# Hybrid attention layer on one core: high and low weight parts laid 128 bytes apart in their buffers

## The chip, the cores and the metric

The kernel runs on one core of a Trainium2 chip. The metric is the time of one execution on the device in microseconds (us), taken as the median of several runs. Engine names: PE is TensorE (matrix products; PEld is its weight load, a separate row of the trace), ACT is ScalarE, DVE is VectorE, POOL is GpSimd, SP issues most DMAs. A matmul has a stationary operand, which PEld loads into the array (128 columns here), and a moving operand, which is streamed through it (256, 272 or 512 columns here).

## What is computed

One decoder layer on x of 256 rows by 1024 columns, all in float32: an input RMS norm, one large product with `w_in` (1024 by 5648), block attention with 8 heads of 64, gated linear attention (GLA) with 4 heads, two branch products `w_proj_a` and `w_proj_b`, gates, the output product `w_out`, a residual and a final RMS norm.

```python
h = rms_norm(x, norm_in_g[layer])
proj = jnp.einsum('bsd,de->bse', h, w_in[layer])
(mq, mk, mv, mgate, gq, gk, gv, ggate, gfg, ga, gb) = jnp.split(proj, split_pts, axis=-1)
...
oa = oa.transpose(0, 2, 1, 3).reshape(B, S, MOBA_WIDTH) * jax.nn.silu(mgate)
ya = jnp.einsum('bse,ed->bsd', oa, w_proj_a[layer])
...
yb = jnp.einsum('bse,ed->bsd', ob, w_proj_b[layer])
merged = (jax.nn.sigmoid(ga + b_merge[layer, 0]) * ya
          + jax.nn.sigmoid(gb + b_merge[layer, 1]) * yb)
x = x + jnp.einsum('bsd,de->bse', merged, w_out[layer])
...
return rms_norm(x, norm_f_g)
```

## The kernel before

Every large product is made of three matmuls in the reduced type fp32r (helper `three`): high part by high part, high by low, low by high. Activations are split once (`xh`, `xl`; later `oah`/`oal`, `obh`/`obl`, `mh`/`ml`). Weights are split as they arrive. A weight matrix is cut into chunks of up to 1056 elements per partition. `load_to` issues a chunk's DMA on SP into one of five `raw` buffers; `split_to` makes `hi` from `raw` on ACT (line 179) and `lo` as `raw` minus `hi` on DVE (line 180), each into one of five ring buffers of `SMAX` = 1088 elements. `prefetch` keeps loads some eight chunks and splits four chunks ahead of the products.

The groups run in this order: `mg`, `gg`, `gqk`, `mq`, `mk`, `mv`, `gv`, `ga0`, `ga1`, `gb0`, `gb1`, `pa0`, `pb0`, `pa1`, `pb1`, and then the output product (`po`). There are four kinds:

- K (`mg`) and F (`gqk`, `mq`, `mk`, `ga`, `gb`, `pa`, `pb`): the weights are stationary (128 columns of `hi` or `lo`), the activations move (256 columns). An F group has two banks; each is 2 x 8 x 3 = 48 matmuls (2 x 4 x 3 = 24 for `pa` and `pb`). The order within a `three` is `hi` with `xh`, `hi` with `xl`, `lo` with `xh`.
- G (`gg`) and T (`mv`, `gv`), and `po`: the activations are stationary, and `hi` or `lo` move, 512 columns at a time (256 and 272 in `gg`, 512 and 256 in `po`).

The side work (GLA, attention, gates, merge) is written as generators; `tick`, called after every second step of an F group, starts the side steps that are due by a clock that `mm` counts from shapes alone. So the order of instructions on every engine is fixed when the kernel is built.

All large buffers lie at addresses that are equal modulo 256 bytes within their kind: every `hi` and `lo` buffer begins at 32 modulo 256 (4352 bytes each, 17 x 256), `xh`, `xl`, `oah`, `oal`, `obh`, `obl` at 224. The `raw` buffers are 4224 bytes (16.5 x 256), so consecutive ones alternate between 32 and 160 modulo 256. A row of a `gg` chunk takes 544 elements (2176 bytes, 8.5 x 256): of its two k steps the first begins at 32 and the second at 160 modulo 256.

Of the kernel before, what the change touches and what calls it, by code (L numbers as in the profile page):

```python
# [22 lines left out]
D = 1024  # L23
# [15 lines left out]
C_MQ, C_MK, C_MV, C_MG = 0, 512, 1024, 1536  # L39
C_GQ, C_GV, C_GG, C_FG, C_GA, C_GB = 2048, 2560, 3072, 3584, 3600, 4624  # L40
RANK = 16


def constants():
# [34 lines left out]
def layer(ctx, tc, x, norm_in_g, w_in, b_merge, w_fg2, b_fg, gla_g, w_pa, w_pb, w_out, norm_f_g,  # L79
# [10 lines left out]
    def mm(out, lhsT, rhs, start, stop):  # L90
        nc.tensor.matmul(out, lhsT, rhs, start=start, stop=stop)  # L91
        n = out.free_size() / 2400
        clock[0] += n if rhs.dtype == F32R else 4 * n

    def transpose(out, in_, identity):
        nc.tensor.transpose(out, in_, identity)
        clock[0] += 0.11

    def f32(ap):
        return ap.bitcast(F32)  # L100
# [11 lines left out]
    chunks = []  # L112
    groups = []

    def group(kind, name, src, c0, n, nk, step=2):
        ids = []
        if kind == "F":
            parts = [(c0 + p, 256, k0, 4) for p in range(0, n, 256) for k0 in range(0, nk, 4)]
        else:
            parts = [(c0, n, k0, step) for k0 in range(0, nk, step)]  # L120
        for c, w, k0, k in parts:
            ids.append(len(chunks))
            chunks.append(dict(src=src, c0=c, n=w, k0=k0, nk=k))
        groups.append(dict(kind=kind, name=name, ids=ids, nk=nk))

    group("K", "mg", w_in, C_MG, 512, KD, 1)
    group("G", "gg", w_in, C_GG, 528, KD)
    group("F", "gqk", w_in, C_GQ, 512, KD)
    group("F", "mq", w_in, C_MQ, 512, KD)
    group("F", "mk", w_in, C_MK, 512, KD)  # L130
# [10 lines left out]
    for half in range(2):  # L141
        for n in range(2):
            for k in range(4 * half, 4 * half + 4, 2):
                oids[n, k // 2] = len(chunks)
                chunks.append(dict(src=w_out, c0=n * 512, n=512, k0=k, nk=2))

    WMAX = 1056
    SMAX = 1088
# [20 lines left out]
    def split_to(n):  # L169
        while done[0] < min(len(chunks), n):  # L170
            c = chunks[done[0]]
            size = c["nk"] * c["n"]
            w = c["n"]
            row = w if w % 32 == 0 else 544
            hi = ring.tile([P, SMAX], F32R, name="hi", bufs=SPLIT)
            lo = ring.tile([P, SMAX], F32R, name="lo", bufs=SPLIT)
            c["hi"], c["lo"] = (t[:, :c["nk"] * row].rearrange("p (k n) -> p k n", n=row)[:, :, :w] for t in (hi, lo))
            raw = c["raw"].rearrange("p (k n) -> p k n", n=w)
            nc.scalar.copy(c["hi"], raw)  # L179
            nc.vector.tensor_sub(c["lo"], raw, f32(c["hi"]))  # L180
            done[0] += 1

    def prefetch(i):

        load_to(i + SPLIT + RAW - 2)
        split_to(i + SPLIT - 1)
# [9 lines left out]
    for k0, k1 in ((0, 1), (1, 2), (2, 4), (4, 6), (6, 8)):  # L196
# [12 lines left out]
        (ggb, gla_g.to_broadcast([P, GDV])),  # L209
        (fgw[0:RANK, :], w_fg2),  # L210
        (fgw[RANK:RANK + 1, :], b_fg),
        (sumsf, sums),
# [64 lines left out]
    for k in range(2):  # L277
        split_to(k + 1)
        x_part(k)
# [15 lines left out]
    kT = one.tile([P, HP, S], F32, name="kT")  # L295
    gfs = one.tile([P, NT, RANK], F32, name="gfs")
    gfT = one.tile([32, S], F32, name="gfT")
# [21 lines left out]
    def give(tag, n=1):  # L319
        room[tag] += n  # L320
# [42 lines left out]
    def gla():  # L363
# [4 lines left out]
        for t in range(NT):  # L368
            transpose(tr[:RANK, t * P:(t + 1) * P], gfs[:, t, :], ident)
        yield 0.6  # L370
        nc.scalar.copy(gfT[:RANK, :], tr[:RANK, :S])
        give("small")
# [3 lines left out]
        for t in range(NT):  # L376
            mm(fg[:, t, :], gfT[:RANK + 1, t * P:(t + 1) * P], fgw[:RANK + 1, :], start=True, stop=True)
        yield 0.8
# [345 lines left out]
    for g in groups:  # L724
        ids, name = g["ids"], g["name"]
        if g["kind"] == "K":
            ps = [small(f"{name}{f}") for f in range(3)] + [bank(f"{name}3", "side", 1)]
            for i in ids:
                c = chunks[i]
                k = c["k0"]  # L730
                if k == 5:
                    squares(0)
                if k == 6:
                    squares(1)
                for f in range(4):
                    fs = slice(f * P, (f + 1) * P)
                    if f == 2:
                        if k + 2 < KD:
                            x_part(k + 2)
                        split_to(i + SPLIT - 1 if k > 3 else i + 3)  # L740
                    three(ps[f][:, :S], c["hi"][:, 0, fs], c["lo"][:, 0, fs], xh[:, k, :], xl[:, k, :],
                          k == 0, k == KD - 1)
            start_side(gates_mg(ps))
        elif g["kind"] == "G":
            ps = {(t, b): (small if t and b else bank)(f"{name}{t}{b}") for t in range(NT) for b in range(2)}
            for i in ids:
                prefetch(i)
                c = chunks[i]
                for kk in range(c["nk"]):
                    k = c["k0"] + kk  # L750
# [8 lines left out]
        elif g["kind"] == "T":  # L759
            ps = [bank(f"{name}{t}") for t in range(NT)]  # L760
            for i in ids:
                prefetch(i)
                c = chunks[i]
                for kk in range(c["nk"]):
                    k = c["k0"] + kk
# [6 lines left out]
        elif g["kind"] == "F":  # L772
            src = {"pa": (oah, oal), "pb": (obh, obl)}.get(name[:2], (xh, xl))
# [18 lines left out]
            nk = g["nk"]  # L792
            per = nk // 4
            for b in range(len(ids) // per):
# [6 lines left out]
                for j in range(2):  # L801
# [3 lines left out]
                    for k in range(nk):  # L805
                        c = chunks[i + k // 4]
# [94 lines left out]
```

## Time and profile before

| | |
|---|---|
| time, median of 3 runs | 209.54 us (209.42 to 210.56) |
| time of the profiled execution | 209.73 us |
| its span, first to last instruction | 208.0 us |
| PE busy | 198.8 us, 96% |
| PEld busy | 182.4 us, 88% |
| DVE, ACT, POOL busy | 141.6, 122.6, 32.5 us |
| granted TensorE clock, mean | 0.997 |

Matmuls overlap in the trace (one is drained while the next streams), so the durations of neighbours add up to more than the time that passed. The pace of a run of matmuls is the distance of two starts, or the length of a piece of the chain divided by its count.

### The profile page before, as it was taken

To read this page: it belongs to the slowest core of one execution; us is meant where nothing else is said; L and a number is where in the kernel's file an instruction comes from. 1 tells how busy PE (TensorE), PEld (TensorE's weight loads), DVE (VectorE), ACT (ScalarE), POOL (GpSimd) and SP (SyncE) were. 2 spreads that over 40 slices of the span, in tenths; PEclk is the share of its full clock that TensorE was granted. 3 is DMA by queue.
4 is the path that set the end of the run, shared out by engine and by line. 5 is a ranking of instruction groups with operands and counts; after the bars stand their busy time and mean duration, and the time that the engine had idled before them with its cause. 6 is when DMAs were issued, how large, how long until landed. Compare 5 with 4: busy or idle time off the path is not lost.

```text
span 208.0 us, 4231 instructions
## 1 busy us (share of the span) xinstructions
PE 198.8 (96%) x1683; PEld 182.4 (88%) x1683; DVE 141.6 (68%) x261; ACT 122.6 (59%) x205; POOL 32.5 (16%) x31
## 2 busy tenths in 40 slices
PE   7999999999999999998999999999999999999970
PEld 2899999899999988775789999999999999989870
DVE  1566778969545899989765556945393959755371
ACT  4369927871999984156775629846455554552251
POOL 2000025800214540103000000200010060420011
PEclk9999999999999999999999999999999999999998
DMA  5999896594364456660343563966344584600022
GB/s 144 349 379 323 238 310 211 135 296 149 101 199 117 145 158 191 193 218 14 107 123 86 182 193 114 294 210 198 108 151 154 168 301 135 204 4 2 0 101 101
DMA packets 28501, 35.39 MB, mean 170 GB/s; under 512 B 1305, under 2 KB 21442, under 8 KB 28482
## 3 DMA queue, kind: packets, MB, share of 16 engines
q1 hardware_dynamic: 28178, 34.60, 54.1%
q10 hardware_dynamic: 304, 0.53, 0.7%
q8 instruction: 13, 0.21, 0.4%
q14 instruction: 6, 0.05, 0.1%
HBM read 34.08 MB, written 1.05 MB: 169 GB/s over the span
## 4 chain that ended last, share of the span: by engine, by line
PE 67%; DVE 11%; ACT 11%; issue 5%; DMA 2%; SPq 1%; POOLq 0%; POOL 0%; ACTq 0%; DVEq 0%
PE ga L91 11%; PE gb L91 11%; PE po L91 8%; PE gg L91 6%; PE gqk L91 6%; PE pa L91 5%; PE pb L91 5%; DVE lo L180 4%; ACT hi L179 4%; PE mg L91 3%; ACT z L700 3%; PE mq L91 3%; DMA xt<-in_x_dram 2%; PE gv L91 2%; DVE EX L417 2%
## 5 line engine op out<-in xcount | busy, mean ns | idle before, releaser
L180 DVE TENSOR_TENSOR lo<-raw,hi 128x1024 fp32r<-128x1024 f32 (+1 forms) x56 | 70.4, 1269 | 23.5 <-ACT hi L179 23.5
L179 ACT CAST hi<-raw 128x1024 fp32r<-128x1024 f32 (+1 forms) x56 | 57.7, 1048 | 21.5 <-PE po L91 6.0
L91 PE MATMUL ga<-xh,hi 128*128 128x256 f32 x64 | 18.1, 283 | 0.0
L91 PE MATMUL gb<-xh,hi 128*128 128x256 f32 x64 | 18.1, 282 | 0.0
L91 PE MATMUL gb<-xh,lo 128*128 128x256 f32 x64 | 17.9, 279 | 0.0
L91 PE MATMUL gb<-xl,hi 128*128 128x256 f32 x64 | 17.9, 279 | 0.0
L91 PE MATMUL ga<-xh,lo 128*128 128x256 f32 x64 | 17.8, 278 | 0.0
L91 PE MATMUL ga<-xl,hi 128*128 128x256 f32 x64 | 17.8, 278 | 0.0
L91 PE MATMUL po<-hi,ml 128*128 128x512 f32 (+1 forms) x40 | 13.9, 347 | 0.0
L91 PE MATMUL po<-lo,mh 128*128 128x512 f32 (+1 forms) x40 | 13.8, 346 | 0.0
L91 PE MATMUL po<-hi,mh 128*128 128x512 f32 (+1 forms) x40 | 13.7, 343 | 0.0
L91 PEld LDWEIGHTS ga<-xh,hi 128*128 128x128 f32 x64 | 12.1, 189 | 0.5 <-issue 0.5
L558 ACT ACTIVATE sm<-sm,mx 128x128 f32<-128x128 f32 (+1 forms) x16 | 7.1, 444 | 8.7 <-DVE mx L553 8.6
L91 PEld LDWEIGHTS gb<-xh,lo 128*128 128x128 f32 x64 | 12.1, 189 | 0.0
L91 PEld LDWEIGHTS gb<-xh,hi 128*128 128x128 f32 x64 | 12.1, 189 | 0.0
L91 PEld LDWEIGHTS ga<-xl,hi 128*128 128x128 f32 x64 | 12.0, 188 | 0.0
L91 PEld LDWEIGHTS gb<-xl,hi 128*128 128x128 f32 x64 | 12.0, 188 | 0.0
L91 PEld LDWEIGHTS ga<-xh,lo 128*128 128x128 f32 x64 | 12.0, 188 | 0.0
L511 POOL TENSOR_TENSOR s<-s,mhalf 128x4 f32<-128x4 f32 x2 | 2.3, 1172 | 54.6 <-DVE s L510 54.6
L624 POOL TENSOR_TENSOR m<-m,sa 128x512 f32<-128x512 f32 x4 | 7.0, 1743 | 23.9 <-DVE m L622 22.0
L91 PE MATMUL mg<-xh,hi 128*128 128x256 f32 x32 | 10.3, 321 | 0.0
L91 PE MATMUL mg<-xl,hi 128*128 128x256 f32 x32 | 9.5, 296 | 0.0
(197 smaller groups left out, 605.7 us busy)
## 6 DMA issues: line engine op xcount, KB each, us to landing
raw<-in_w_in_dram SPq DMA_DIRECT2D x36, 512.0 KB, 3.7
raw<-in_w_out_dram SPq DMA_DIRECT2D x8, 512.0 KB, 4.8
raw<-in_w_in_dram SPq DMA_DIRECT2D x4, 528.0 KB, 6.0
first<-in_w_in_dram SPq DMA_DIRECT2D x8, 256.0 KB, 5.5
raw<-in_w_proj_a_dram SPq DMA_DIRECT2D x4, 512.0 KB, 3.5
raw<-in_w_proj_b_dram SPq DMA_DIRECT2D x4, 512.0 KB, 4.4
xt<-in_x_dram SPq DMA_DIRECT2D x3, 256.0 KB, 5.7
late<-in_norm_f_g_dram SPq DMA_DIRECT2D x1, 512.0 KB, 5.0
```

Of the source, the lines that this page charges most:

```text
L91: nc.tensor.matmul(out, lhsT, rhs, start=start, stop=stop)
L179: nc.scalar.copy(c["hi"], raw)
L180: nc.vector.tensor_sub(c["lo"], raw, f32(c["hi"]))
L417: nc.vector.tensor_mul(e, e, halves(src, LEVELS[l], which))
L511: nc.gpsimd.tensor_tensor(s4, s4, mhalf, op=OP.pow)
L558: nc.scalar.activation(sm[i][:, cs], sm[i][:, cs], AF.Exp, bias=mx[:, i, t:t + 1], scale=0.125, accum_out=den[:, i, t:t + 1])
L624: nc.gpsimd.tensor_add(m, m, cut(sg["ga"]))
L700: nc.scalar.copy(z[i:i + 32], p2[i ^ 32:(i ^ 32) + 32])
```

## The change

Two offsets are given to each chunk, in elements, for `hi` and for `lo`: (0, 32) is kind A, (32, 0) is B, (0, 0) is C and (32, 32) is D; 32 elements are 128 bytes. Groups `gqk`, `mk`, `ga1` get A; `mq`, `ga0` get B; `gb0` and `gb1` alternate A and B from chunk to chunk; `gv` gets D; `mg`, `gg`, `mv`, `pa`, `pb` and the output product stay at C. The buffers keep their size and place; only the views `c["hi"]` and `c["lo"]`, which ACT and DVE write and PE reads, begin 128 bytes later. No instruction is added, removed or moved.

```diff
+KINDS = {'gqk': 'A', 'mq': 'B', 'mk': 'A', 'ga0': 'B', 'ga1': 'A', 'gb0': 'M', 'gb1': 'M', 'gv': 'D'}
+
+
+def shift(name, n):
+    kind = KINDS.get(name, "C")
+    if kind == "M":
+        kind = "AB"[n % 2]
+    return dict(A=(0, 32), B=(32, 0), C=(0, 0), D=(32, 32))[kind]
...
-            chunks.append(dict(src=src, c0=c, n=w, k0=k0, nk=k))
+            chunks.append(dict(src=src, c0=c, n=w, k0=k0, nk=k, shift=shift(name, len(chunks))))
...
-                chunks.append(dict(src=w_out, c0=n * 512, n=512, k0=k, nk=2))
+                chunks.append(dict(src=w_out, c0=n * 512, n=512, k0=k, nk=2, shift=(0, 0)))
...
-            c["hi"], c["lo"] = (t[:, :c["nk"] * row].rearrange("p (k n) -> p k n", n=row)[:, :, :w] for t in (hi, lo))
+            c["hi"], c["lo"] = (t[:, d:d + c["nk"] * row].rearrange("p (k n) -> p k n", n=row)[:, :, :w]
+                                for t, d in zip((hi, lo), c["shift"]))
```

## Rows read from the trace of the kernel before

**Rows 1.** Page: busy time, share of span, instructions; chain's shares by engine.
```profile
PE 198.8 (96%) x1683; PEld 182.4 (88%) x1683; DVE 141.6 (68%) x261; ACT 122.6 (59%) x205; POOL 32.5 (16%) x31
PE 67%; DVE 11%; ACT 11%; issue 5%; DMA 2%; SPq 1%; POOLq 0%; POOL 0%; ACTq 0%; DVEq 0%
```

**Rows 2.** Chain that ended last, in order of time: start us, us, what, count.
```profile
33.38 2.83 PE gqk L91 x24
...
46.16 5.67 PE mq L91 x48
...
51.85 0.58 ACT z L700
...
75.11 1.21 DVE lo L180
...
107.26 7.02 PE ga L91 x60
...
116.53 7.50 PE ga L91 x66
...
125.72 7.26 PE ga L91 x60
132.99 5.66 PE gb L91 x48
138.64 0.44 PE tr L96 x4
139.08 7.51 PE gb L91 x66
146.59 1.78 PE o L91 x16
148.38 9.19 PE gb L91 x78
157.57 0.44 PE tr L96 x4
158.00 5.46 PE pa L91 x48
163.46 5.44 PE pb L91 x48
```

**Rows 3.** Groups by form, 109.36 to 113.8 us: shapes, count, busy us, mean ns.
```profile
L91 PE MATMUL ga<-xh,hi 128*128 128x256 f32 x14 | 3.9, 276 | 0.0
```

**Rows 4.** The same view, 126.5 to 132.8 us.
```profile
L91 PE MATMUL ga<-xh,hi 128*128 128x256 f32 x18 | 5.1, 281 | 0.0
L91 PEld LDWEIGHTS ga<-xh,hi 128*128 128x128 f32 x18 | 3.5, 192 | 0.0
```

**Rows 5.** Timeline of PE, start us and duration us: where each gg k step begins.
```profile
22.24 0.29 PE L91 MATMUL gg<-hi,xh 128*128 128x256 f32 x1
...
23.69 0.28 PE L91 MATMUL gg<-hi,xh 128*128 128x256 f32 x1
...
25.16 0.28 PE L91 MATMUL gg<-hi,xh 128*128 128x256 f32 x1
...
26.60 0.28 PE L91 MATMUL gg<-hi,xh 128*128 128x256 f32 x1
...
28.06 0.28 PE L91 MATMUL gg<-hi,xh 128*128 128x256 f32 x1
```

**Rows 6.** Views of lines 180 and 179: duration ns min/median/max, first, last start us.
```profile
L180 DVE TENSOR_TENSOR lo<-raw,hi x56: 1207/1218/2309, 19.5 to 191.2; 128x1024 fp32r<-128x1024 f32 x52, 128x1056 fp32r<-128x1056 f32 x4
L179 ACT CAST hi<-raw x56: 1029/1049/1073, 18.4 to 190.1; 128x1024 fp32r<-128x1024 f32 x52, 128x1056 fp32r<-128x1056 f32 x4
```

**Rows 7.** Waits by engine and line: us in total, times, longest us.
```profile
DVE lo L180 <- ACT hi L179: 25.9, 19, 3.6
```

## The prediction

> **What bounds the kernel now.** I read the page's busy times first and then the chain that ended last. PE is busy for 96% of the span, and two thirds of the chain is PE's [rows 1]. In order of time the chain has three parts [rows 2]. Up to about 52 us it is PE: `mg`, `gg`, `gqk` and the first bank of `mq`. Then it passes to ACT at the first eviction of `mq` (51.85) and to DVE (one of its splits stands at 75.11), and stays there until the GLA and attention work of that stretch is through. From about 96 us to the end of `po` it is PE again, through `ga`, `gb`, `pa`, `pb`. So a nanosecond saved in a matmul counts in the first and the last part, and is given back as a wait in the middle.
>
> Next I divided the chain's PE pieces by their counts, because the change touches only where operands lie. All these matmuls have the same shape: 128 weight columns loaded, 256 columns streamed. They run at two paces. `pb` takes 5.44 us for 48, 113.3 ns each; `pa` is the same but for its first one. `gqk` takes 2.83 for 24, 117.9; `mq` 5.67 for 48, 118.1; the first piece of `gb` 5.66 for 48, 117.9; its last 9.19 for 78, 117.8. The middle piece of `gb` takes 7.51 for 66, 113.8 with its start included [rows 2]. The view by form shows the same from another side: a `ga` matmul of the quick pace lasts 276 ns, one of the slow pace 281, and in the slow stretch the load of one of the three operands lasts 192 ns instead of 188 [rows 3, 4]. I call the difference a step: 117.8 - 113.3 = 4.5 ns.
>
> What changes the pace? Not the clock (0.997 over the span), not the buffers (a run of 48 or more crosses several chunks, whose buffers rotate), and not ACT or DVE, since `pb` holds 113.3 while splits run beside it. The pace changes only where side matmuls come between: after the `tr` at 138.64 `gb` is quick, after the `o` at 146.59 slow, after the `tr` at 157.57 `pa` is quick and stays so [rows 2]. Within a run it stays, after the first few. So it looks like two ways for weight load and moving stream to fall into step with each other, or with something that serves both, and the start decides which.
>
> **Does a shift of 128 bytes matter to that?** The trace has one place where it is tried. In `gg` the moving operand starts at 32 modulo 256 in one k step and at 160 in the next. From 22.24 a step at 160 takes 1.45 us, then 1.47 at 32, 1.44 at 160, 1.46 at 32 [rows 5]: 12 matmuls are about 0.02 us shorter at 160, some 1.5 ns each, a third of a step. So PE is not blind to these 128 bytes. That is the moving operand; in the F groups it is the stationary one that the change moves, and no row tries that.
>
> **The change, part by part.**
>
> PE, F groups (kinds A, B, M). No instruction, wait or DMA is added, so the count on each queue and the order on each engine stay. In the kernel before, all three weight loads of a `three` stand in the same relation to what is streaming: weights at 32, activations at 224, modulo 256. With A the `lo` load stands 128 bytes off, one of three; with B the two `hi` loads do. A pace in which each of the three pays a step needs each to meet the same relation; with one of them moved off, I expect the slower pace to break up and the stream to fall to the quick pace, as it does by itself after some breaks. The price of that:
> - `gqk`, 96 matmuls (pieces of 24, 24 and 48 in the chain; one row stands for them), and the first bank of `mq`, 48: 144 x 4.5 ns = 0.65 us, on the path because ACT's eviction at 51.85 waits for the end of that bank [rows 2].
> - `ga` from 125.72, 60 matmuls (7.26 us: 60 at 117.8 and about 0.2 us to start), and `gb`, 48 and 78: 186 x 4.5 = 0.84 us, on the path [rows 2].
> - The quick runs (`ga` 60 at 107.26 and 66 at 116.53, `gb` 66 at 139.08; 192 matmuls) are taken to stay quick: nothing.
> - The rest of `mq` and `mk` (144 at the slower pace) lie in the ACT and DVE part: PE gets there up to 0.65 us sooner and waits. I take nothing, and keep 0.65 us as the far end should the side work follow.
>
> PE, `gv` (kind D). `hi` and `lo` move together, which is what `gg` does between its k steps: 48 matmuls x 1.5 ns = 0.07 us either way by that row, and the stage is in DVE's part of the chain, so nothing.
>
> ACT and DVE. They write and read `hi` and `lo` 128 bytes on. `raw` alternates by just these 128 bytes from buffer to buffer against `hi` and `lo`, and the median split on DVE lasts 1218 ns with a fastest of 1207, on ACT 1049 between 1029 and 1073 [rows 6]: no second level shows. (The longest on DVE, 2309 ns, are a few isolated ones.) I take nothing and keep 0.1 us both ways, since DVE's splits already wait 25.9 us in all for ACT's [rows 7] and so have slack outside the middle part. DMAs land in `raw`, which does not move.
>
> The sum is 0.65 + 0.84 = 1.49 us. The quick runs too start with a few slow matmuls (60 in 7.02 us is 0.22 us over 60 x 113.3), so I take nine tenths, 1.34 us. The profiled execution took 209.73 us, 0.19 above the median of 209.54; from its own time the sum gives 208.39, from the median 208.2. The forecast is 208.2.
>
> **A rule that speaks against the change.** The paces above are what the rows show [rows 2]. The Trainium skill, page "SBUF — State Buffer", section "Who interferes with whom", says that PE has two independent read ports, one for the moving operand and one for weight loads, and that "PE and ACT never wait on anyone". By that the place of the weights could cost PE nothing and the time would stay at 209.5. The `gg` steps speak against its strict reading; for stationary operands no row here shows it either way. It is the second case below. The page "TensorE: Matmul & The Clock Gate", section "Wait — 56ns, not 53.3ns?", puts the distance of two warm starts at N / 2.4 GHz plus about 2.5 ns; as an estimate by that page that is 109.2 ns for 256 columns, and all 522 matmuls on the path at it would give about 205.9 us. No row here shows a 256-column pace under 113.3.
>
> **The rivals.**
> 1. The shift doesn't do what it is laid out for: the pace hangs on the moving operand and on how a run starts, and the weights' place is of no matter. For it: buffers of all addresses show both paces, and a break alone changes them [rows 2]. Against it: the load that lasts 192 ns instead of 188 at the slower pace, so the weight side takes part [rows 4]. Then runs start as before, or are dealt anew: if the share of quick runs stays, 209.5; all 192 quick ones turned slow would cost 0.86 us, 210.4.
> 2. The moved relation is the dearer one. Then each load that stands 128 bytes off pays a step more, at either pace alike. A moves one of three, B two of three, about half over the groups: half of 144 + 186 + 192 = 522 is 261 x 4.5 ns = 1.17 us, 210.7. It decides from 1.05 us, that is 233 loads that pay. For it: the one row on the shift shows that the two relations differ by a third of a step [rows 5], and in `gg` that is for better from 32 to 160 against 224, which says nothing of the other operand. Against it: `pa` and `pb` run at 113.3 in the old relation, so that one is not dear in itself, and the new one would have to be dear at every start.
> 3. Only the front gains, because `ga` and `gb` are dealt anew at each of their breaks: 0.65 us, 208.9. This lies within the bound of what can be told from no change, and is counted there.
>
> **How the numbers follow.** About 0.5% (1.05 us) is what a measurement of this kernel can tell from no change. The forecast has 0.50, rivals 1 and 3 together 0.38, rival 2 has 0.12. Faster by over 0.5% (under 208.5) is the forecast, 0.50; within it 0.38; slower 0.12. The forecast's own range is 207.2 to 208.6: its low end is 209.54 less 1.49, less the 0.65 of `mq` and `mk`, less 0.07 of `gv` and 0.1 of ACT and DVE. The whole range goes from 207.2 to 210.0; it leaves out rival 2 and the upper part of rival 1.
>
> **What would show it.** In the changed profile I would divide the same chain pieces by their counts. Right: `gqk` and `mq` at 113 to 114 ns, each piece of `ga` and `gb` likewise, durations of 276 ns instead of 281, ACT's first eviction of `mq` near 51.2 instead of 51.85, `gv` and the splits as before. Wrong in the mechanism: `gqk` still at 118, so that weights' addresses don't matter; wrong in place: the front quicker and the end no earlier, if ACT or DVE takes the gain; wrong in sign: matmuls of 256 columns above 118 ns, or loads above 192. Since the pace is set anew at each break, a gain in some pieces and a loss in others is the result that would hurt the forecast most.

## The result and the profile after

The changed kernel takes 211.0 us (median of 14 runs, 209.76 to 212.44) beside 209.81 us for the kernel before in the same comparison (14 runs): a ratio of 1.0055, interval 1.003 to 1.008. Two more comparisons, told below, gave 1.0014 (0.998 to 1.0048) and 1.0039 (1.0019 to 1.0059). So the change makes the kernel slower, by 0.1 to 0.6%, which one of the three comparisons can't tell from no change; the forecast was 208.2. The profiled execution took 210.74 us, its span is 208.9, and the granted clock 0.997, as before.

The page's busy times of after (engine, busy us, share of the span, instructions) stand against [rows 1]:

```profile
PE 199.2 (95%) x1683; PEld 182.7 (87%) x1683; DVE 142.6 (68%) x261; ACT 122.4 (59%) x205; POOL 37.2 (18%) x31
```

The same instructions, and the sums hardly differ. What differs is in the chain that ended last, in order of time (start us, us, what, count). After:

```profile
33.92 2.75 PE gqk L103 x24
...
36.90 2.77 PE gqk L103 x24
...
40.73 5.65 PE gqk L103 x48
46.38 5.45 PE mq L103 x48
...
51.85 0.58 ACT z L713
...
96.86 3.69 PE gv L103 x15
...
102.77 1.41 PE gv L103 x6
...
107.34 7.33 PE ga L103 x60
...
116.93 7.68 PE ga L103 x66
...
126.31 7.01 PE ga L103 x60
133.32 5.44 PE gb L103 x48
138.76 0.44 PE tr L108 x4
139.20 7.54 PE gb L103 x66
146.73 1.78 PE o L103 x16
148.52 8.91 PE gb L103 x78
157.42 0.44 PE tr L108 x4
157.86 5.66 PE pa L103 x48
163.51 5.65 PE pb L103 x48
...
180.48 16.75 PE po L103 x84
```

Divided by their counts and held against [rows 2], these rows tell the whole result. `mq` fell from 118.1 to 113.5 ns, the last piece of `ga` from 7.26 to 7.01 us, the first and the last piece of `gb` from 5.66 to 5.44 and from 9.19 to 8.91: the forecast gains are there. But the first piece of `ga`, quick before, rose from 7.02 to 7.33, and `pa` and `pb`, whose weights the change doesn't touch, rose from 113.3 to 117.8 ns (5.66 for 48). `gv` and `po` grew too; these are their rows in the chain of before:

```profile
96.86 3.64 PE gv L91 x15
...
102.72 1.38 PE gv L91 x6
...
179.78 16.47 PE po L91 x84
```

To add this up I take PE's timeline from the first `gg` matmul to the end of the last `po` one, because the start-up ahead of it differs from run to run by more than the change is worth: over the profiles of this study `gg` begins between 19.9 and 22.2 us. Timeline of PE (start us, duration us, what), first and last matmul of that stretch, before and then after:

```profile
20.45 0.28 PE L91 MATMUL gg<-hi,xh 128*128 128x256 f32 x1
...
201.43 0.28 PE L91 MATMUL po<-hi,ml 128*128 128x256 f32 x1
```

```profile
20.97 0.28 PE L103 MATMUL gg<-hi,xh 128*128 128x256 f32 x1
...
202.40 0.28 PE L103 MATMUL po<-hi,ml 128*128 128x256 f32 x1
```

That is 181.25 us before and 181.71 after (by the times in ns), 0.46 us longer; the other 0.5 us between the two spans is `gg` beginning 0.51 us later. Behind the last `po` matmul both spans have about 6.25 us left. By stages, each from the first start of one operation to that of the next:

| stretch | before, us | after, us | difference |
|---|---|---|---|
| first `gg` to ACT's first eviction of `mq` | 31.40 | 30.89 | -0.51 |
| to the first `ga` | 52.08 | 52.16 | +0.08 |
| to `gb` | 28.89 | 29.14 | +0.25 |
| to `pa` | 24.94 | 24.46 | -0.48 |
| to `po` | 21.86 | 22.70 | +0.84 |
| to the end of PE | 22.08 | 22.37 | +0.28 |

The +0.25 of `ga` is a gain of 0.25 (its last piece) and a loss of 0.50 (the first two). So 1.24 us were gained, and 1.70 lost: `ga` 0.50, `gv` 0.08, `pa` and `pb` 0.84, `po` 0.28.

The loss in `ga` can be seen to end with the kind. The piece of 66 holds the last 30 matmuls of `ga0` (kind B) and the first 36 of `ga1` (kind A), with nothing between them. In PE's timeline they come 118.9 ns apart up to the first of `ga1`, and 113.3 from its seventh on.

ACT and DVE have no part in it. Their splits of the large chunks in the changed kernel (duration ns min/median/max, first and last start us) are those of [rows 6] within 2 ns at the median:

```profile
L193 DVE TENSOR_TENSOR lo<-raw,hi x56: 1208/1219/2323, 20.0 to 192.1; 128x1024 fp32r<-128x1024 f32 x52, 128x1056 fp32r<-128x1056 f32 x4
...
L192 ACT CAST hi<-raw x56: 1030/1050/1072, 18.9 to 191.0; 128x1024 fp32r<-128x1024 f32 x52, 128x1056 fp32r<-128x1056 f32 x4
```

### The profile page after: what moved, and what is told of

Same layout as the page of the kernel before. It is cut to its first block, busy times and chain, and to the rows that moved or that the text cites. A ratio compares the mean times of both kernels' runs of the same rounds, so it can differ in the third digit from the quotient of the medians.

```text
span 208.9 us, 4231 instructions
## 1 busy us (share of the span) xinstructions
PE 199.2 (95%) x1683; PEld 182.7 (87%) x1683; DVE 142.6 (68%) x261; ACT 122.4 (59%) x205; POOL 37.2 (18%) x31
## 4 chain that ended last, share of the span: by engine, by line
PE 68%; ACT 11%; DVE 11%; issue 5%; DMA 2%; SPq 0%; POOLq 0%; POOL 0%; DVEq 0%; ACTq 0%
PE ga L103 11%; PE gb L103 10%; PE po L103 8%; PE gg L103 6%; PE pb L103 5%; PE pa L103 5%; PE gqk L103 5%; DVE lo L193 4%; PE mg L103 4%; ACT hi L192 4%; ACT z L713 3%; PE mq L103 3%; PE gv L103 2%; DVE EX L430 2%; DMA xt<-in_x_dram 2%
## 5 line engine op out<-in xcount | busy, mean ns | idle before, releaser
L193 DVE TENSOR_TENSOR lo<-raw,hi 128x1024 fp32r<-128x1024 f32 (+1 forms) x56 | 71.5, 1288 | 24.7 <-ACT hi L192 24.7
L717 POOL TENSOR_TENSOR kT<-kT,z 128x512 f32<-128x512 f32 x2 | 10.5, 5246 | 7.2 <-DVE z L716 7.2
L637 POOL TENSOR_TENSOR m<-m,sa 128x512 f32<-128x512 f32 x4 | 6.0, 1502 | 25.4 <-DVE m L635 23.3
```

Source lines behind the costliest of these rows:

```text
L637: nc.gpsimd.tensor_add(m, m, cut(sg["ga"]))
L717: nc.gpsimd.tensor_add(dst, dst, z)
```

## Experiments

Two questions were open: why groups that nothing was done to became slower, and whether the paces are a property of a kernel or are dealt anew in each execution. All experiments are edits of `KINDS`, on the changed kernel unless said otherwise; "C" is the place of before. I call 113.3 ns per matmul of 256 columns the quick pace and 117.8 the long one. The measure is the stretch from the first `gg` matmul to the end of PE, 181.25 us before and 181.71 after; profiles of one kernel agree in it within 0.06 us. Where a kernel was timed, the ratio to the kernel before stands beside it. B everywhere, D everywhere, `gb` back at C and the front alone were executed once each and rest on this stretch and the chain.

**The same two kernels again.** No edit.

> The changed kernel once more, for a second profile. Theory (the pace of a run of 256-column matmuls is chosen where the run starts, 113.3 or 117.8 ns each; groups with one part moved come to 113.3, unmoved ones stay as they began): gqk at 113 to 115 again, ga0 about 118.9 again, but pa, pb and po may begin otherwise: 48 of pb in 5.44 or in 5.65 us, and the time differs from 210.7 by up to 1.1 us with it. Rival (the moved parts set everything that follows, the same in each execution): pb at 5.65 for 48 again and the time within 0.3 us of 210.7.

> The kernel before once more, one look. Theory: gqk, mq and mk can begin at either pace, pb too; the stretches at 113.3 and at 117.8 need not be those of the first profile. Rival (the layout alone sets the pace): the same pieces at the same pace as in the first profile, pb 5.44 for 48, gqk 5.65 to 5.85 for 48.

The changed kernel again: 181.67 us; the kernel before again: 181.24. In each of the two pairs the pieces of the chain have the same lengths to 0.02 us, `pa` at 5.66 and at 5.46 among them. The times: 210.28 us, ratio 1.0014 (0.998 to 1.0048). My theory that each start of a run deals the pace by chance fell here: a kernel has its paces, piece by piece.

**`pa` and `pb` moved too.**

```diff
-KINDS = {..., 'gv': 'D'}
+KINDS = {..., 'gv': 'D', 'pa0': 'A', 'pb0': 'A', 'pa1': 'A', 'pb1': 'A'}
```

> pa and pb are also given kind A, nothing else is changed. Theory: pa and pb come to 113.3 in a few matmuls whatever their start, pb 5.44 to 5.5 us for 48, and the time is 0.85 us (192 x 4.45 ns) below the changed kernel's, 209.6 to 210.2, with less spread from execution to execution. Rival (the tail is slower for another reason, contention or the order of work): pa and pb stay at 5.65 for 48 and the time near 210.9.

180.58 us, 1.13 less than the changed kernel where 0.85 was expected; 208.83 us at the median of 5 runs, ratio 0.9958 (0.9905 to 1.0011). Everything up to the last `tr` is as in the changed kernel; behind it the chain reads:

```profile
148.75 8.91 PE gb L103 x78
157.65 0.44 PE tr L108 x4
158.09 5.46 PE pa L103 x48
...
179.87 16.47 PE po L103 x84
```

The end is that of before again, and with it `po` (16.47), which this edit doesn't touch. So the 0.28 us of `po` were not its own: it is longer when the run ahead of it is at the long pace.

**Kind A, B or D everywhere.** In each, `mg` and all groups with stationary weights get one kind, and `gv` goes back to C.

```diff
+KINDS = dict.fromkeys(('mg', 'gqk', 'mq', 'mk', 'ga0', 'ga1', 'gb0', 'gb1', 'pa0', 'pb0', 'pa1', 'pb1'), 'A')
```

> Kind A for mg and all groups with stationary weights, kind C for the rest (gv too). Theory: no run stays at 117.8; ga0 comes to 113.3 where kind B held it at 118.9 (about 110 matmuls x 5.5 ns = 0.6 us less than in tail_A), mg's later steps too (1.36 us for 12 instead of 1.42): 208.3 to 209.2. Rival (a gain of one group is paid by the next): some of the groups at 118 or above, 209.8 or more.

A everywhere: 179.97 us, 1.28 less than before; 208.35 us at the median of 4 runs, ratio 0.9908 (0.9875 to 0.9941). Its chain:

```profile
106.58 7.01 PE ga L103 x60
...
115.84 7.52 PE ga L103 x66
...
125.05 7.01 PE ga L103 x60
132.07 5.44 PE gb L103 x48
...
147.27 8.86 PE gb L103 x78
156.12 0.44 PE tr L108 x4
156.56 5.49 PE pa L103 x48
162.05 5.44 PE pb L103 x48
```

No piece here is left at the long pace. `pa` begins slowly (from its second to its tenth matmul they come 117 to 124 ns apart in the timeline) and then falls to 113.3; in the changed kernel `pa`, at C, begins at the long pace and stays there.

> Kind B (hi moved) for mg and every group with stationary weights, C for the rest. Theory (A leaves one pace, 113.3; B has a second that holds, 118.9, and the phase at a group's start decides): ga0 from gv at 118.9 again (7.33 us for 60), and it is not left until a break; groups entered from a run at 113.3 stay there; first gg to end of PE above all_A's 179.97 us by 0.5 to 3 us. Rival (118.9 in ga0 came from gv's kind D ahead of it, not from B): with gv at C ga0 runs at 113.3 like under A, 7.02 for 60.

B everywhere: 182.04 us, 0.79 more than before. The pieces of `ga`, the last two of `gb` and the first of `pa` in its chain:

```profile
106.99 7.33 PE ga L103 x60
...
116.57 7.85 PE ga L103 x66
...
126.11 7.33 PE ga L103 x60
...
139.59 7.51 PE gb L103 x66
...
148.88 9.27 PE gb L103 x78
...
158.59 5.45 PE pa L103 x48
```

The piece of 66 is at 7.85 / 66 = 118.9 ns, the last of `gb` at 118.9: a pace of B's own, longer than the long one. `ga`'s 7.33 for 60 is the same as in the changed kernel, where this first part of `ga` is B too; with A it takes 7.01. `gv`, just ahead, is D in the changed kernel and C here, so it isn't the cause. So the loss in `ga` is the price of its kind. Yet B's `pa` is at 113.3, and so is its `gb` for 66 matmuls, until a break after which the last 78 are at 118.9. `mq` too, B in both kernels and with no break ahead, is at 118.9 here, behind a `gqk` at that pace, and at 113.3 in the changed kernel, behind a quick `gqk`. So B can hold either of two paces, and a break can change which.

> Kind D (hi and lo both moved) for mg and every group with stationary weights, C for the rest. Theory (what matters is that one part stands otherwise than the other): D is like C, some stretches hold 117.8 to their end (gqk 48 in 5.65 or more), others 113.3; first gg to end of PE 181 to 182.5 us, like before's 181.25 and the changed kernel's 181.70. Rival (what matters is that weights and activations stand otherwise to each other than before): no stretch holds 117.8, 180.0 us as with all_A.

D everywhere: 181.66 us. Of its chain:

```profile
139.48 7.77 PE gb L103 x66
...
149.04 9.19 PE gb L103 x78
...
158.67 5.45 PE pa L103 x48
```

The last `gb` and `pa` are as at C, but `gb` between the two breaks is at 117.7 ns where C has 7.51. With D, `hi` and `lo` stand together and only their relation to the activations is new. Like C it holds either pace and mends neither. So what takes the long pace away is `hi` and `lo` standing 128 bytes apart, and of the two orders only A's leaves the quick pace alone.

**`gb` back at C.**

```diff
-KINDS = {..., 'ga1': 'A', 'gb0': 'M', 'gb1': 'M', 'gv': 'D'}
+KINDS = {..., 'ga1': 'A', 'gv': 'D'}
```

> The changed kernel with gb0 and gb1 back at kind C. Theory (pa's pace is set by the phase in which gb and the four transposes leave PE): gb, entered from ga1 at 113.3, holds that up to its first break and then takes either pace as in the kernel before; where its last piece runs at 117.8 (9.19 us for 78), pa and pb go at 113.3 (5.44 for 48), where at 113.3, at 117.8 (5.65). Rival (the tail is slower because something ahead of gb is moved): pa and pb at 5.65 whatever gb does.

180.84 us. In its chain the last run of `gb` is at the long pace again, and `pa` and `pb`, at C as in the changed kernel, at the quick one:

```profile
133.11 5.44 PE gb L103 x48
...
138.99 7.51 PE gb L103 x66
...
148.28 9.19 PE gb L103 x78
157.47 0.44 PE tr L108 x4
157.91 5.45 PE pa L103 x48
163.37 5.44 PE pb L103 x48
...
179.69 16.47 PE po L103 x84
```

Only the group ahead was changed, and 0.84 us came back in `pa` and `pb`, 0.28 in `po`. So the loss in these three groups comes from `gb`'s kind. The four transposes between take 0.44 us in both; what differs is the kind of `gb` and with it the pace at which PE comes to them. Left at 117.8 (before, D, this one) or 118.9 (B), `pa` begins quick; left at 113.3 in the changed kernel, it begins long and at C stays so for 192 matmuls. With `pa` at A the same entry is mended, within its first few matmuls behind the changed kernel's `gb` and after its tenth in A everywhere.

That the pace ahead is what decides is not shown, though, and the break in the middle of `gb` speaks against it as a rule. Four transposes stand there too. At C `gb` comes to them at 117.8 in the kernel before (5.66 for 48) and at 113.3 here (5.44), and both times the 66 behind take 7.51; D comes at 117.7 and goes on at 117.7. What of the entry decides stays open.

**The front alone.**

```diff
-KINDS = {'gqk': 'A', 'mq': 'B', 'mk': 'A', ...}
+KINDS = {'gqk': 'A', 'mq': 'B', 'mk': 'A'}
```

> Only gqk, mq and mk are moved as in the changed kernel; ga, gb and gv are at C. Theory: first gg to the first eviction of mq 30.9 us instead of 31.4, as in the changed kernel; the middle ends at DVE and ACT, so ga starts in the phase it had before and takes the paces of the kernel before piece by piece (60 in 7.02, 66 in 7.50, 60 in 7.26), pb 5.44 for 48: 0.5 us below before over all, 181.25 to 180.75 from first gg to end of PE. Rival (each gain up front is paid back behind): ga, gb or pa take other paces and the end is within 0.2 us of before's 181.25 or later.

180.71 us, 0.54 less than before. From `ga` on its pieces are those of [rows 2] to 0.02 us (7.02, 7.50, 7.26, 5.66, 7.51, 9.19, 5.46). So the gain of the front isn't given back in the middle part, and doesn't upset the end; the upset comes from what is moved behind it, `ga`, `gb` and `gv`.

**Timed again, and `po`.** The changed kernel and A everywhere once more, beside 30 runs of the kernel before; then A everywhere with the output weights moved as well:

```diff
-                chunks.append(dict(src=w_out, c0=n * 512, n=512, k0=k, nk=2, shift=(0, 0)))
+                chunks.append(dict(src=w_out, c0=n * 512, n=512, k0=k, nk=2, shift=(0, 32)))
```

and with `(32, 0)` in its place.

> The changed kernel a third time, timed beside all_A on one chip. Two profiles of it agree piece by piece from the first gg on and put it 0.45 us above the kernel before over that stretch. Theory (that is the whole loss, the rest of the 1.2 us of the first comparison is the spread of the start): a ratio of 1.001 to 1.004 to the kernel before. Rival (other executions take other paces than the profiled ones): 1.005 or more, as in the first comparison, and this profile has a piece at another pace.

> Kind A on every group with stationary weights, again, with more rounds. Theory: 1.28 us less than the kernel before from the first gg to the end of PE, in each execution: a ratio of 0.991 to 0.996. Rival (its first ratio of 0.9908 was a lucky draw): 0.998 or more.

> all_A with the lo parts of the output weights moved as well; they are the moving operand there. Theory (the same lock in another place): the 512-column matmuls of po change their pace, 84 in another time than 16.47 us, down to 16.3 if they come to twice 113.3. Rival (po is bound by streaming, the place of its operands does not matter): 16.47 us for 84.

> all_A with the hi parts of the output weights moved instead of the lo parts. Theory: another pace again, two of three streams stand otherwise; 16.3 to 16.8 us for 84. Rival (no matter): 16.47 us for 84.

| kernel | first `gg` to end of PE, us | `po` in the chain, 84 | median, us (runs) | ratio, interval |
|---|---|---|---|---|
| changed, third time | 181.65 | 16.75 | 210.47 (12) | 1.0039 (1.0019 to 1.0059) |
| A everywhere, again | 179.97 | 16.47 | 208.69 (7) | 0.9963 (0.9931 to 0.9996) |
| and `po` at A | 180.31 | 16.67 | 208.76 (10) | 0.9957 (0.9933 to 0.998) |
| and `po` at B | 180.35 | 16.71 | 209.23 (10) | 0.9988 (0.9959 to 1.0017) |

The changed kernel has the same paces for the third time, A everywhere for the second; the latter's 0.9963 lies just above the 0.991 to 0.996 expected. In `po` the weights move and the activations are stationary; there either shift costs 0.2 us or more, where kind A was thought able to bring 16.3, so it stays at C. A everywhere beats both kernels in its two comparisons.

How far do paces and times agree? 0.46 us of 209.8 is a ratio of 1.002 for the changed kernel, and -1.28 is 0.994 for A everywhere. Both intervals of A hold 0.994; two of the three of the changed kernel hold 1.002, and the first, 1.003 to 1.008, doesn't. So of the 1.2 us between the first two medians 0.46 is shown to be PE's pace; the rest is not. The start of `gg`, which differs by 2.3 us over all profiles, is large enough for it, but whether it lies later with this change isn't settled: in three profiles it lies at 20.97, 20.10 and 22.20 us, in two of the kernel before at 20.45 and 20.79.

## Why the prediction was wrong

- **What bounds the kernel: right.** PE's pace counts in the first and last part; [rows 1, 2] have their like after, and the gain of the front reached the end (moved alone, PE ends 0.54 us sooner). That ACT's first eviction of `mq` stands at 51.85 in both chains is chance: `gg` began 0.51 us later.
- **Two paces that the weights' place can change: right**, against the first rival. `gqk`, `mq`, the last piece of `ga` and two of `gb` went quick as forecast. The Trainium skill, page "SBUF — State Buffer", section "Who interferes with whom", says that "PE and ACT never wait on anyone"; what the prediction drew from it, that the place of the weights could cost PE nothing, isn't so here: 128 bytes in that place change PE's pace by 4.5 ns a matmul at one clock, with ACT's and DVE's work the same. No run shows that PE waits on another engine for it, so the sentence itself is not refuted.
- **The size of the gain: nearly.** 1.24 us of 1.49, against 1.34 taken. The front gave 0.51 of 0.65, in the main because runs of 24 have hardly settled when they end (2.83 to 2.75, and to 2.77, where 24 x 4.5 ns would be 0.11); `ga` and `gb` gave 0.73 of 0.84.
- **"The quick runs are taken to stay quick: nothing": this step failed**, for 0.5 us. `ga`'s first part got kind B, which has a pace of 118.9 of its own; B everywhere and A everywhere show it from both sides. The reason given, that a slow pace needs all three loads in one relation, made A and B alike, and they aren't: A with one of three moved brought every long run shown here to 113.3, B with two can hold 118.9 for a whole run.
- **`pa`, `pb` and `po` weren't costed at all, and that is the larger failure**, 1.12 us. They stay at C, so I counted them as untouched, and the 522 matmuls counted as on the path leave out the 192 of `pa` and `pb`. But the prediction had read from [rows 2] that only breaks change the pace, and that `pa` became quick at one. Then what PE does ahead of the break can decide what `pa` does behind it, and a change of `gb` can change `pa`; with `gb` back at C alone, `pa`, `pb` and `po` are as before. The 0.86 us of the first rival (192 matmuls turned slow) was this loss, in the other place, and was given to the case in which the weights don't matter.
- **`gv`: the size was right and its place wrong.** I put it into DVE's part of the chain, but its rows stand in both chains as PE's. D costs 0.08 us there, near the 0.07 either way that was worked out from [rows 5] and then left out.
- **The second rival** had the right sign and the wrong mechanism: the moved relation isn't dearer by itself, since A everywhere has it in every run with stationary weights and is the quickest kernel here. Only for B does it have a dearer pace, 118.9, which is the sign that the prediction named (256 columns above 118 ns), and B shows 113.3 as well.
- **Durations as a sign: poor.** I would have told the paces by 276 and 281 ns [rows 3, 4]. It held for `pa` and `pb`, whose `hi` load also lasts 192 ns at the long pace (by form, line, engine, operands, shapes, count, busy us and mean ns, 159 to 168 us of after, and behind it 126.5 to 132.8 us):

```profile
L103 PEld LDWEIGHTS pa<-oah,hi 128*128 128x128 f32 x12 | 2.3, 192 | 0.0
...
L103 PE MATMUL pa<-oah,hi 128*128 128x256 f32 x13 | 3.7, 281 | 0.0
```

```profile
L103 PE MATMUL ga<-xh,hi 128*128 128x256 f32 x19 | 5.4, 282 | 0.0
```

But this last row is of a kind A run at the quick pace (7.01 for 60). Under another layout the duration of one matmul doesn't tell the pace; the length of a piece over its count does.

## What to carry to other kernels

A pace that PE holds through a run of matmuls can hang on how the run is entered, so an edit that touches one run has to be costed in the runs behind it, the untouched ones first. Where a layout only holds whichever pace it finds, look for one that falls into the quick pace by itself (here `lo` 128 bytes on, and `hi` left in its place), and use it for all runs of that form and for no other form. Compare two builds by one stretch of the timeline as well as by their times, when the start-up varies by more than the edit is worth.

## What the runs showed of the hardware

The paces belong to the kernel and not to the execution: three profiles of the changed kernel, two of the one before and two of A everywhere have each piece of the chain at the same length to 0.02 us or so, though `gg` begins up to 2 us apart.

A `three` takes 340.0 ns at the quick pace (`pb` of before) and 353.3 at the long one; two of them take 713.3 ns at B's; and one of 512 columns takes 686.7 ns in `po`. These times, worked out from starts in ns, are 51, 53, 107 and 103 times 6.667 ns; nine matmuls of 512 columns take 2073.3 ns with `po` at A and 2080.0 at B, 311 and 312 times that. Single distances (117 to 119 ns at the long pace) are no whole multiples. It looks as if weight loads and moving operands keep to a common beat of that length, and the pace were the number of beats that a layout and an entry need; that is argued from the numbers and not shown by an experiment. The Trainium skill, page "TensorE: Matmul & The Clock Gate", section "Wait — 56ns, not 53.3ns?", makes the distance of two starts 109.2 ns as an estimate for 256 columns; no layout tried here brought these groups under 113.3.
